# Neighbourhood attention: the probabilities are normalised by VectorE's tensor_scalar with an accumulated sum

## The chip, the cores and the metric

The kernel runs on one core of one Trainium2 chip. The metric is the time of one execution on the device in microseconds (us). Matmuls run on TensorE (PE in the profile, its weight loads PEld), elementwise work on VectorE (DVE), ScalarE (ACT) and GpSimd (POOL), and transfers are issued mostly by SyncE (SP). Matmul results land in PSUM, everything else lies in the on-chip buffer SBUF.

## The reference

Two layers of a transformer with two parallel mixers. Each layer projects the normalised and modulated tokens (512 latent tokens on a grid of 8 rows by 64 columns, and 256 context tokens) by one matrix, and runs two attentions of 8 heads each; both are gated, projected, merged and projected again. The change touches the first of the two, the neighbourhood attention, in which a latent query reads a window of 8 rows by 16 columns around it, and all 256 context keys:

```python
s_win = jnp.einsum('bchd,bicjhd->bhcij', qr, kw).astype(jnp.float32) * scale + bias[None]
s_ctx = jnp.einsum('bchd,blhd->bhcl', qr, kc).astype(jnp.float32) * scale
s = jnp.concatenate([s_win.reshape(B, NA_HEADS, GRID_W, wr * WIN_C), s_ctx], axis=-1)
p = jax.nn.softmax(s, axis=-1).astype(v.dtype)
```

The output is p times the values. In layer 0 the context tokens have queries too, which read the 256 context keys by an ordinary softmax; in layer 1 they have none.

## The kernel before, in words

All is fp32. A projection splits both factors into a high part that the fast matmul form keeps exactly and a low remainder, and multiplies three times: high by high, high by low, low by high (`mm3`, L435 to L437). The split of the weights costs a cast on ScalarE (L405, L420) and a subtraction on GpSimd or VectorE (L408, L422).

The neighbourhood attention goes head by head, 8 heads in a layer (`pipeline`, `na_first`, `na_scores`). For a head, keys and queries are staged first: `stage_k` (L866 to L868; the low part of the keys, `kl`, on GpSimd) and `stage_q` (L877 and L878; the low part of the queries, `qs`, on VectorE from two operands in SBUF). Then come four blocks of 128 queries by 512 columns, 256 for the window and 256 for the context. In each of them

- two matmuls give the scores in PSUM (L884, L885, or L972),
- VectorE adds the bias, negates, and writes the minimum beside the tile into the first column of `mx` (L975); its bias tile holds zeros in the context half,
- ScalarE takes the exponential and writes its sum into `r` (L978),
- `softmax_tail` turns `r` into its reciprocal on VectorE (L788) and multiplies p by it and by the constant P_UP = 2^14. For blocks 0 and 2 VectorE does both in one instruction over the tile (L795). For blocks 1 and 3 (NA_ACT) VectorE multiplies the 128x1 `r` by P_UP (L790), and ScalarE multiplies the tile (L793),
- `turned` splits the context half into two fp16 parts, on ScalarE (L835) and GpSimd (L836), and a transposing transfer of SyncE (L840) turns them.

Layer 0 has one more piece for each head: `ctx_scores` with `late` False, 2 x 128 context queries by 256 keys, which calls `softmax_tail` for two columns of `r` and two pieces of 256 columns, always on VectorE (two L795 for one L788). The call with `late` True, in the second attention, doesn't normalise there.

One head behind, `na_values` multiplies by the values: the window halves of p are turned on TensorE (L803, L805), evacuated in two fp16 parts (`transpose_split`, L811 on ScalarE and L812 on VectorE), and multiplied (L996 to L1006); `head_out` adds the two halves of the result (L825, L826) and multiplies it into the gate tile on GpSimd (L827).

Between the heads, `pipeline` runs pieces of gate projections (`fill`), which are matmuls of the `mm3` kind with their evacuations (L623, L625). They need nothing of the attention, and keep TensorE at work while a softmax is under way.

The order of the instructions on each engine is not the order of the code: the tile framework's planner lists them by its own estimate of when each could start, after the whole program is known. Some short runs are held together by hand (`behind`). An engine then works through its own list strictly in order.

The pool tiles concerned are `p` (8 buffers), `mx` (128x2, 8 buffers) and `r` (128x2, 8 buffers).

Of the kernel before, what the change touches and what calls it, by code (L numbers as in the profile page):

```python
# [12 lines left out]
ALU = mybir.AluOpType  # L13
# [20 lines left out]
NA_ACT = (1, 3)  # L34
P_UP = 2.0 ** 14
# [37 lines left out]
def hybrid_kernel(es: ExitStack, tc, x, ctx, cvec, w_ada, w_ada0, small, gvec, w_in, w_o_a, w_o_b, w_out,  # L73
                  bias_int, bias_edge, rope, ident_d, out):
    nc = tc.nc
    V, S, G, T = nc.vector, nc.scalar, nc.gpsimd, nc.tensor
# [10 lines left out]
    def nm(s):  # L87
        uid[0] += 1
        return f"{s}_{uid[0]}"
# [398 lines left out]
    def run(fill, n):  # L488
        for _ in range(min(n, len(fill))):
            fill.pop(0)()  # L490
# [102 lines left out]
    def layer(l, hx, nxt, start):  # L593
# [189 lines left out]
        bgp_es.close()  # L783

        if True:
            def softmax_tail(p, n, r, pieces, on_act=False):

                V.reciprocal(r, r)  # L788
                if on_act:
                    V.tensor_scalar(r, r, P_UP, None, ALU.mult)  # L790
                for i, (c0, c1) in enumerate(pieces):
                    if on_act:
                        S.activation(p[:, c0:c1], p[:, c0:c1], AF.Copy, scale=r[:, i:i + 1])  # L793
                    else:
                        V.tensor_scalar(p[:, c0:c1], p[:, c0:c1], r[:, i:i + 1], P_UP, ALU.mult, ALU.mult)  # L795

            def transpose_split(blocks, n0=0, n1=512):

# [30 lines left out]
            def turned(p, n, out, eng):  # L829

                if att["w"] == 512 and n == 512:
                    h = att["p"].tile([128, 2, n], F16, tag="hc", name=nm("hc"), bufs=1)
                else:
                    h = att["p"].tile([128, 2, n], F16, tag="h", name=nm("h"), bufs=att["nh"])
                S.copy(h[:, 0], p[:, :n])  # L835
                eng.tensor_tensor(h[:, 1], p[:, :n], h[:, 0], ALU.subtract)  # L836
                if not isinstance(out, list):
                    out = [(out, 0, 128)]
                for o, n0, n1 in out:
                    nc.sync.dma_start_transpose(o, h[n0:n1].rearrange("p a n -> p (a n)"))  # L840
# [40 lines left out]
            def scores(ps, q, kh, kl, cuts):  # L881

                for c0, n, sl in cuts:
                    T.matmul(ps[:, c0:c0 + n], q, sl(kh), start=True, stop=False)  # L884
                    T.matmul(ps[:, c0:c0 + n], q, sl(kl), start=False, stop=True)  # L885

            def cut(a, b):
                return lambda k: k[:, a:b]

            def ctx_scores(q, kh, kl, ct, late=True):  # L890

                pss = ps_score()
                for i in range(2):
                    scores(pss, q[:, 512 + 128 * i:640 + 128 * i], kh, kl,
                           [(256 * i, 256, cut(512, 768))])
                mx = sp.tile([128, 2], F32, tag="mx", name=nm("mx"), bufs=8)
                V.tensor_reduce(mx, pss.rearrange("p (i n) -> p i n", i=2), AX, ALU.max, negate=True)
                if late:
                    V.tensor_scalar(mx, mx, P_LOG, None, ALU.add)
                p = p_tile()  # L900
                r = sp.tile([128, 2], F32, tag="r", name=nm("r"), bufs=8)
                for i in range(2):
                    S.activation(p[:, 256 * i:256 * i + 256], pss[:, 256 * i:256 * i + 256], AF.Exp,
                                 bias=mx[:, i:i + 1], accum_out=r[:, i:i + 1])
                if not late:
                    softmax_tail(p, 512, r, [(0, 256), (256, 512)])
                turned(p, 512, ct.rearrange("p a i k n -> p (a i k) n"), G)
                return ct, r

# [13 lines left out]
            def p_tile():  # L923
                return att["p"].tile([128, att["w"]], F32, tag="p", name=nm("p"), bufs=att["np"])

            def ps_score(n=512):
                return psw(n, "s")
# [18 lines left out]
            def load_bias(h):  # L946
                nc.sync.dma_start(bint[:, 0:256], bias_int[l, h])
                for i in range(2):
                    nc.sync.dma_start(bedg[64 * i:64 * i + 64, 128 * i:128 * i + 128],
                                        bias_edge[l, h, 64 * i:64 * i + 64])  # L950
# [3 lines left out]
            def na_scores(h, q, kh, kl):  # L954
                load_bias(h)
                ps_ = []
                ht = turns[:, 2048 * (h % 2):2048 * (h % 2) + 2048].rearrange("p (g n) -> p g n", g=4)
                for i in range(4):
                    pss = ps_score()
                    qi = q[:, 128 * i:128 * i + 128]  # L960
                    if i == 0:
                        scores(pss, qi, kh, kl, [(0, 128, cut(0, 128)), (128, 384, cut(384, 768))])
                    else:
                        o = 128 * (i - 1)
                        step = 512 - o

                        def sl(k, o=o, step=step):
                            a = k[:, o:o + 256]
                            return bass.AP(tensor=a.tensor, offset=a.offset,
                                           ap=[a.ap[0], [step, 2], [1, 256]])  # L970
                        for kk, b in ((kh, True), (kl, False)):
                            T.matmul(pss.rearrange("p (s n) -> p s n", s=2), qi, sl(kk), start=b, stop=not b)  # L972
                    p = p_tile()
                    mx = sp.tile([128, 2], F32, tag="mx", name=nm("mx"), bufs=8)
                    V.tensor_tensor_reduce(p[:, :512], pss, bedg if i == 0 else bint, -1.0, 3e38,  # L975
                                           ALU.add, ALU.min, mx[:, 0:1])
                    r = sp.tile([128, 2], F32, tag="r", name=nm("r"), bufs=8)
                    S.activation(p[:, :512], p[:, :512], AF.Exp, bias=mx[:, 0:1], scale=-1.0,  # L978
                                 accum_out=r[:, 0:1])
                    softmax_tail(p, 512, r[:, 0:1], [(0, 512)], i in NA_ACT)  # L980
                    at = [(0, 64, 0), (448, 512, 64)] if i == 0 else [(128 * i - 64, 128 * i + 64, 0)]
                    turned(p[:, 256:512], 256, [(ht[:, :, a:b], n, n + b - a) for a, b, n in at], G)
                    ps_.append(p)
                    run(att["bg"], 1)
                return ps_, ht
# [46 lines left out]
            def na_first(h):  # L1032
                j, e = h // 2, h % 2
                kh, kl = akt[e]
                stage_k(kav[:, j, :], e, kh, kl, False)
                q = stage_q(qav[:, j, :], e)
                st = na_scores(h, q, kh, kl)
                if not first:
                    return st, None
                o = 4096 + 1024 * (h % 2)  # L1040
                ct = turns[:, o:o + 1024].rearrange("p (a i k n) -> p a i k n", a=2, i=2, k=2)
                return st, ctx_scores(q, kh, kl, ct, False)
# [126 lines left out]
            def gq_first(h):  # L1169
                kh, kl = gkt[h // 4]  # L1170
                q = stage_q(qbv[:, h // 2, :], h % 2)
                ht = gq_scores(q, kh, kl)
                if not first:
                    return ht, None
                if h % 2 == 0:
                    ct = vbig[:, 2432:2944].bitcast(F16).rearrange("p (a i k n) -> p a i k n", a=2, i=2, k=2)
                else:
                    ct = att["p"].tile([128, 2, 2, 2, 128], F16, tag="ct", name=nm("ct"), bufs=1)
                return ht, ctx_scores(q, kh, kl, ct)
# [336 lines left out]
```

## Time and profile before

| | us |
|---|---|
| median of three runs | 1127.05 |
| the three runs | 1122.82, 1127.42, 1127.05 |
| the profiled execution, its own time | 1125.0 |
| the profiled execution, first to last instruction (span) | 1122.9 |
| neighbourhood attention of layer 0 in it, about | 150 to 285 |
| neighbourhood attention of layer 1 in it, about | 770 to 880 |

The mean granted TensorE clock of the profiled execution is 0.992 of full speed. A row of a group reads: line, engine, operation, tile written <- tiles read, shapes, count, then busy us, mean ns of one, and the idle time of the engine before them with what ended it. A row of the order of time reads: start, duration, engine, line, and in brackets the idle time before it with what ended it. An instruction's duration may overlap the next one's by a little, so the distance from one start to the next (the step) is often shorter than the duration.

### The profile page before, as it was taken

What the parts mean: (1) busy time and instruction counts of PE and PEld (TensorE: products, weight loads), DVE (VectorE), ACT (ScalarE), POOL (GpSimd) and SP (SyncE); (2) the same over time, 40 slices, a digit from 0 to 9 for tenths busy, and PEclk for the clock granted to TensorE, in tenths of its full rate; (3) what the DMA queues carried; (4) which work ended last, traced back from release to release, by engine and by line L of the source; (5) the groups of instructions that cost most, each with busy time, mean ns of one, the idle gap of its engine ahead of it and who ended that gap; (6) DMA issues with size and microseconds to landing.
All of it is one profiled execution on the core that took longest, in us unless ns stands there. A gap on an engine that the chain in (4) does not pass through costs nothing. (4 is left out here: it accounts for less than half of the span.)

```text
span 1122.9 us, 16871 instructions
## 1 busy us (share of the span) xinstructions
PE 1079.4 (96%) x5672; PEld 876.5 (78%) x5672; DVE 761.7 (68%) x1496; ACT 616.7 (55%) x1236; POOL 497.0 (44%) x413
## 2 busy tenths in 40 slices
PE   8999998999999999969999999999999999999998
PEld 5687887888888877757788788888776888776677
DVE  5667889874377478775577785466987565677473
ACT  6464278876333566655330275445997346777431
POOL 1044355655247244454521445233665473564531
PEclk9999998999999999989999999999999999999999
DMA  9454324555543497769524542453556436879742
GB/s 369 150 169 143 91 70 95 137 136 124 170 127 127 127 203 187 170 183 263 181 96 126 178 132 81 138 162 94 118 134 144 136 111 165 205 229 229 196 146 80
DMA packets 235999, 171.79 MB, mean 153 GB/s; under 512 B 160140, under 2 KB 201864, under 8 KB 234248
## 3 DMA queue, kind: packets, MB, share of 16 engines
q1 hardware_dynamic: 228576, 156.31, 51.5%
q0 software_dynamic: 2368, 7.87, 2.2%
q10 hardware_dynamic: 4968, 6.53, 1.8%
q8 instruction: 45, 0.74, 0.3%
q14 instruction: 42, 0.34, 0.1%
HBM read 115.58 MB, written 17.32 MB: 118 GB/s over the span
## 5 line engine op out<-in xcount | busy, mean ns | idle before, releaser
L836 POOL TENSOR_TENSOR h<-p,h 128x256 f16<-128x256 f32 (+2 forms) x104 | 112.5, 1090 | 144.3 <-ACT h L835 106.7
L435 PE MATMUL psf<-hx,whi 128*128 128x512 f32 (+1 forms) x360 | 137.8, 383 | 1.2 <-ACT zt L623 1.2
L422 POOL TENSOR_TENSOR wlo<-raw,whi 128x512 fp32r<-128x512 f32 x70 | 97.4, 1396 | 93.8 <-ACT whi L420 55.9
L437 PE MATMUL psf<-hx,wlo 128*128 128x512 f32 (+1 forms) x360 | 135.2, 376 | 0.0
L436 PE MATMUL psf<-hx,whi 128*128 128x512 f32 (+1 forms) x360 | 135.1, 375 | 0.0
L435 PE MATMUL psx<-whi,hx 128*128 128x512 f32 (+1 forms) x328 | 120.9, 372 | 0.0
L437 PE MATMUL psx<-whi,hx 128*128 128x512 f32 (+1 forms) x328 | 120.1, 367 | 0.0
L436 PE MATMUL psx<-wlo,hx 128*128 128x512 f32 (+1 forms) x328 | 119.6, 366 | 0.0
L420 ACT CAST whi<-raw 128x512 fp32r<-128x512 f32 x136 | 82.0, 619 | 62.8 <-DMA raw<-in_w_in_dram 40.3
L408 POOL TENSOR_TENSOR wlo<-raw,whi 128x512 fp32r<-128x512 f32 x40 | 59.6, 1493 | 123.9 <-ACT whi L405 78.1
L405 ACT CAST whi<-raw 128x512 fp32r<-128x512 f32 x88 | 54.5, 624 | 104.6 <-PE psx L437 34.2
L506 POOL TENSOR_TENSOR ss<-ss,ehalf 128x8 f32<-128x8 f32 (+2 forms) x40 | 63.1, 1580 | 79.4 <-DVE ss L503 74.2
L422 DVE TENSOR_TENSOR wlo<-raw,whi 128x512 fp32r<-128x512 f32 x66 | 69.5, 1054 | 36.5 <-ACT whi L420 35.0
L835 ACT CAST h<-p 128x256 f16<-128x256 f32 (+2 forms) x136 | 81.3, 616 | 11.4 <-DMA ct<-h 5.1
L1147 DVE CUSTOM_DVE_ANT_0 p<-pss,vb 128x768 f32<-128x768 f32 x64 | 60.3, 954 | 27.3 <-PE pss L885 23.8
L435 PEld LDWEIGHTS psf<-hx,whi 128*128 128x128 f32 x360 | 67.9, 188 | 13.6 <-ACT zt L623 2.3
L1148 ACT ACTIVATE p<-pss,mx 128x768 f32<-128x768 f32 x64 | 57.6, 900 | 36.1 <-DVE mx L1147 35.1
L437 PEld LDWEIGHTS psf<-hx,wlo 128*128 128x128 f32 x360 | 67.8, 188 | 12.0
L436 PEld LDWEIGHTS psf<-hx,whi 128*128 128x128 f32 x360 | 67.9, 189 | 10.5
L437 PEld LDWEIGHTS psx<-whi,hx 128*128 128x128 f32 x328 | 62.0, 189 | 10.3
L436 PEld LDWEIGHTS psx<-wlo,hx 128*128 128x128 f32 x328 | 62.0, 189 | 9.5
L435 PE MATMUL psx<-hx,whi 128*128 128x256 f32 (+1 forms) x208 | 69.0, 332 | 0.0
(337 smaller groups left out, 2986.2 us busy)
## 6 DMA issues: line engine op xcount, KB each, us to landing
raw<-in_w_in_dram SPq DMA_DIRECT2D x168, 256.0 KB, 3.0
rawb<-in_w_ada_dram SPq DMA_DIRECT2D x48, 256.0 KB, 2.7
raw<-in_w_out_dram SPq DMA_DIRECT2D x32, 256.0 KB, 2.9
tg<-gs SPq DMA_DIRECT2D x4, 1536.0 KB, 6.9
rawx<-in_w_ada_dram SPq DMA_DIRECT2D x4, 1024.0 KB, 10.3
rawy<-in_w_ada_dram SPq DMA_DIRECT2D x4, 1024.0 KB, 9.8
gs<-zt ACTq DMA_DIRECT2D x16, 256.0 KB, 2.7
raw<-in_w_o_a_dram SPq DMA_DIRECT2D x16, 256.0 KB, 3.1
```

The lines of the kernel that those rows point to most:

```text
L405: S.copy(hi[:, :n], raw[:, :n])
L408: e.tensor_tensor(lo[:, :n], raw[:, :n], F(hi[:, :n]), ALU.subtract)
L420: S.copy(hi, raw)
L422: lo_eng(i).tensor_tensor(lo, raw, F(hi), ALU.subtract)
L435: T.matmul(ps, lhs[0], rhs[0], start=first, stop=False)
L436: T.matmul(ps, lhs[0], rhs[1], start=False, stop=False)
L437: T.matmul(ps, lhs[1], rhs[0], start=False, stop=last)
L506: G.tensor_tensor(ss, ss, ehalf[:, :n], ALU.pow)
L835: S.copy(h[:, 0], p[:, :n])
L836: eng.tensor_tensor(h[:, 1], p[:, :n], h[:, 0], ALU.subtract)
L1147: V.tensor_tensor_reduce(p, pss, lift, -1.0, 3e38, ALU.add, ALU.min, mx[:, 0:1])
L1148: S.activation(p, pss, AF.Exp, bias=mx[:, 0:1], accum_out=r[:, i:i + 1])
```

## The change

`softmax_tail` gets the tile `mx` as one more argument, called `total`. Where VectorE normalises, the constant P_UP no longer stands in the instruction over the tile: `r` is multiplied by it beforehand, by the small instruction that the calls for ScalarE already had. The instruction over the tile multiplies by `r` and adds 0.0, and its form also writes the sum of what it writes along the row into the second column of `mx`, which nothing reads. Nothing else differs; blocks 1 and 3 are as they were.

```diff
-            def softmax_tail(p, n, r, pieces, on_act=False):
+            def softmax_tail(p, n, r, total, pieces, on_act=False):
 
                 V.reciprocal(r, r)
-                if on_act:
-                    V.tensor_scalar(r, r, P_UP, None, ALU.mult)
+                V.tensor_scalar(r, r, P_UP, None, ALU.mult)
                 for i, (c0, c1) in enumerate(pieces):
                     if on_act:
                         S.activation(p[:, c0:c1], p[:, c0:c1], AF.Copy, scale=r[:, i:i + 1])
                     else:
-                        V.tensor_scalar(p[:, c0:c1], p[:, c0:c1], r[:, i:i + 1], P_UP, ALU.mult, ALU.mult)
+                        V.tensor_scalar(p[:, c0:c1], p[:, c0:c1], r[:, i:i + 1], 0.0, ALU.mult, ALU.add,
+                                        accum_out=total[:, 1:2])
...
                 if not late:
-                    softmax_tail(p, 512, r, [(0, 256), (256, 512)])
+                    softmax_tail(p, 512, r, mx, [(0, 256), (256, 512)])
...
-                    softmax_tail(p, 512, r[:, 0:1], [(0, 512)], i in NA_ACT)
+                    softmax_tail(p, 512, r[:, 0:1], mx, [(0, 512)], i in NA_ACT)
```

## The prediction

> **What bounds the kernel now.** I read the page's first part, then the busy time by stretches of the two places where the changed function runs, then TensorE's waits there, and last the order of time around the longest of them.
>
> ```profile
> span 1122.9 us, 16871 instructions
> PE 1079.4 (96%) x5672; PEld 876.5 (78%) x5672; DVE 761.7 (68%) x1496; ACT 616.7 (55%) x1236; POOL 497.0 (44%) x413
> 150.00:285.00 135.00, 131.24 (x791) 111.56 (x790) 103.94 (x229) 104.40 (x238) 79.72 (x81) 0.97 0.51 120
> 770.00:880.00 110.00, 103.29 (x534) 80.12 (x533) 86.26 (x191) 89.32 (x191) 64.14 (x58) 1.00 0.51 129
> ```
>
> The first two lines are the page's; the other two are stretches (start and end, length, then busy time of PE, PEld, DVE, ACT, POOL, granted clock, share and rate of DMA): the neighbourhood attention of layer 0 and of layer 1. TensorE bounds the kernel: it is busy for 96% of the span. VectorE's time counts only where it makes TensorE wait or lose its clock. In these two stages TensorE has 135.00 - 131.24 = 3.8 us and 110.00 - 103.29 = 6.7 us without a matmul: all that the change can win at once.
>
> Next, the changed instruction (L795), by shape and by its longest wait; the last line stands under "who waited for it":
>
> ```profile
> L795 DVE TENSOR_SCALAR p<-p,r x48: 340/487/3866, 155.6 to 861.3; 128x512 f32<-128x512 f32 x32, 128x256 f32<-128x256 f32 x16
> L795 DVE TENSOR_SCALAR p<-p,r 128x512 f32<-128x512 f32 x32 | 26.9, 842 | 1.0
> L795 DVE TENSOR_SCALAR p<-p,r 128x256 f32<-128x256 f32 x16 | 7.1, 488 | 0.2
> 150.00:285.00 135.00, 19.19 (x32) 0.97 0.51 120
> 770.00:880.00 110.00, 14.82 (x16) 1.00 0.51 129
>   PE pst L805: 3.2, 1
> ```
>
> Fastest, median and slowest are 340, 487 and 3866 ns, and the mean of the 512-wide ones, 842 ns, is far above their median: some of them stand still in the middle. (The two rows of stretches count L795's VectorE time alone.) What they stand still for shows in the order of time, of VectorE, GpSimd and TensorE:
>
> ```profile
> 178.21 4.13 DVE L795 TENSOR_SCALAR p<-p,r 128x256 f32<-128x256 f32 x2
> 178.10 1.58 POOL L827 TENSOR_TENSOR za<-za,ho 64x512 f32<-64x512 f32 x1 [3.00 <-DMA bedg<-in_bias_edge_dram]
> 179.66 1.16 POOL L836 TENSOR_TENSOR hc<-p,hc 128x512 f16<-128x512 f32 x1
> 180.78 1.27 POOL L422 TENSOR_TENSOR wlo<-raw,whi 128x512 fp32r<-128x512 f32 x1
> 185.36 1.83 POOL L868 TENSOR_TENSOR kl<-ka,kh 64x768 fp32r<-64x768 f32 x1 [1.78 <-PE psf L437]
> 187.15 1.26 POOL L422 TENSOR_TENSOR wlo<-raw,whi 128x512 fp32r<-128x512 f32 x1
> 185.91 3.31 DVE L878 TENSOR_TENSOR qs<-qa,qs 64x768 fp32r<-64x768 f32 x1
> 203.05 0.95 DVE L878 TENSOR_TENSOR qs<-qa,qs 64x768 fp32r<-64x768 f32 x1
> 189.25 0.49 DVE L795 TENSOR_SCALAR p<-p,r 128x512 f32<-128x512 f32 x1
> 189.80 0.48 PE L805 MATMUL pst<-ident,p 128*128 128x128 f32 x1 [3.19 <-DVE p L795]
> 190.84 0.58 PE L996 MATMUL psv<-ht,va 128*128 128x512 f16 x1 [0.57 <-DVE r L790]
> 188.00:190.00 2.00, 0.20 (x1) 0.20 (x2) 1.97 (x3) 1.98 (x8) 0.41 (x1) 0.78 0.00 0
> 190.00:192.00 2.00, 1.43 (x4) 0.48 (x4) 1.97 (x8) 1.79 (x5) 1.13 (x2) 0.50 0.18 35
> 192.00:194.00 2.00, 2.00 (x11) 1.34 (x9) 2.00 (x3) 1.01 (x3) 1.75 (x3) 0.50 0.69 228
> 194.00:196.00 2.00, 2.00 (x12) 2.00 (x11) 1.97 (x8) 1.82 (x5) 1.52 (x3) 0.52 0.65 169
> 196.00:198.00 2.00, 2.00 (x18) 1.96 (x18) 0.91 (x2) 1.88 (x5) 1.40 (x3) 1.00 0.82 207
> ```
>
> (A row merges equal neighbours, hence 4.13 us for two.) L795 ends when three GpSimd instructions in a row have ended; then L878, with two operands in SBUF, is held by two more (3.31 us, against 0.95 us when nothing was in its way). The p that follows is late, TensorE stands for 3.19 us, then 0.57 us more, and the granted clock falls to 0.50 until 196. This stall costs 3.2 + 0.6 + (2.0 - 0.57) x 0.50 + 2.0 x 0.50 + 2.0 x 0.48 = 6.5 us, though only 3.8 us of it show as idle.
>
> **The change part by part.** *Removed:* the fast L795. Undisturbed, its step to the next instruction is 0.41 us at 512 columns, and a pair at 256 takes 0.53 us:
>
> ```profile
> 155.62 0.48 DVE L795 TENSOR_SCALAR p<-p,r 128x512 f32<-128x512 f32 x1
> 156.03 0.16 DVE L788 RECIPROCAL r<-r 128x1 f32<-128x1 f32 x1
> 156.22 0.15 DVE L790 TENSOR_SCALAR r<-r 128x1 f32<-128x1 f32 x1
> 156.29 0.41 DVE L625 SCALAR_TENSOR_TENSOR za<-za,psx 128x256 f32<-128x256 f32 x1
> 156.66 0.69 DVE L422 TENSOR_TENSOR wlo<-raw,whi 128x512 fp32r<-128x512 f32 x1
> 163.16 0.62 DVE L795 TENSOR_SCALAR p<-p,r 128x256 f32<-128x256 f32 x2
> 163.69 0.15 DVE L788 RECIPROCAL r<-r 128x1 f32<-128x1 f32 x1
> ```
>
> At medians of 0.487 and 0.340 us, layer 0's 16 + 16 would take 13.2 us and not 19.19, layer 1's 16 would take 7.8 us and not 14.82: 6.0 and 7.0 us are waiting.
>
> *Added, the form with a sum.* Its time isn't in this trace. The nearest rows are the mask-and-minimum of the same stage, which writes a minimum beside its tile and is followed by a read of it, and a reduction whose input lies in SBUF:
>
> ```profile
> 153.60 0.68 DVE L975 CUSTOM_DVE_ANT_0 p<-pss,bedg 128x512 f32<-128x512 f32 x1
> 154.22 0.08 DVE L975 DVE_READ_ACCUMULATOR2_ANT mx<- 128x1 f32 x1
> 154.22 0.68 DVE L975 CUSTOM_DVE_ANT_0 p<-pss,bint 128x512 f32<-128x512 f32 x1
> L503 DVE TENSOR_REDUCE ss<-sq 128x8 f32<-128x520 f32 x32 | 21.8, 688 | 7.0 <-ACT sq L502 6.8
> ```
>
> Below, the new form may stay at the step of 0.41 us; above, it takes 0.69 + 0.08 = 0.77 us one behind the other. I take 0.62, the step of L975 with its read, since that is the row that does the same two things: + 0.21 us each. At 256 columns the nearest is L625's step, 156.66 - 156.29 = 0.37, against 0.53 / 2 = 0.27: + 0.10 us. Layer 0: 16 x 0.21 + 16 x 0.10 = 5.0 us; layer 1: 16 x 0.21 = 3.4 us.
>
> *Added, the small multiply* (r by P_UP, L790's kind), once for each call that normalises on VectorE: 16 + 8 in layer 0, 16 in layer 1. L790's step is 0.07 us where the next instruction needs nothing of it. Here the next one reads r, and then a dependent step counts: 0.19 us, as from L788 to L790 above. 24 x 0.07 to 0.19 = 1.7 to 4.6 us, and 16 x 0.07 to 0.19 = 1.1 to 3.0 us.
>
> *What goes with it.* If the new form doesn't take what GpSimd holds, the 6.0 and 7.0 us of waiting go. VectorE's sum is then 5.0 + (1.7 to 4.6) - 6.0 = + 0.7 to + 3.6 us in layer 0, and 3.4 + (1.1 to 3.0) - 7.0 = - 2.5 to - 0.6 us in layer 1: neutral, with the gain where waits are long. The sum written into mx's second column has no reader; it is written behind both exponentials, on the engine that writes mx anyway. Queued behind L795 on VectorE are the next tiles' L975, for which ScalarE's exponentials wait. No DMA is added or moved.
>
> [...]
>
> *On TensorE.* Up to 182 us layer 0 has five L795 of 512 columns and four of 256, with seven multiplies: VectorE is 5 x 0.21 + 4 x 0.10 + 7 x (0.07 to 0.19) = 1.9 to 2.8 us longer, partly absorbed where it now waits. I let 1.3 us of it arrive. The two L795 at 178.21 take 4.13 us; without the wait they would take 0.74, so 3.4 us go. The stall of 3.2 us becomes about 3.2 - 3.4 + 1.3 = 1.1 us, too short for the clock to fall if it goes as with the stands of 0.6 and 0.8 us in layer 1:
>
> ```profile
> 813.17 0.33 PE L884 MATMUL pss<-kh,qs 128*128 128x128 f32 x1 [0.59 <-DVE mx L975]
> 814.63 0.44 PE L805 MATMUL pst<-ident,p 128*128 128x128 f32 x2 [0.80 <-ACT p L793]
> 814.00:816.00 2.00, 1.36 (x7) 1.21 (x8) 1.94 (x6) 1.95 (x3) 0.26 (x1) 1.00 0.33 106
> ```
>
> That is 6.5 - 1.1 = 5.4 us won (0 to 6.5). Layer 1: VectorE is 0.6 to 2.5 us shorter, and a part of 6.7 us idle follows it: 1.3 us won (0 to 6.7). Layer 0 after the stall: VectorE longer, TensorE mostly covered by the gate projections queued there: 0.5 us lost (0 to 3.6). Sum: - 5.4 - 1.3 + 0.5 = - 6.2 us.
>
> The profiled execution took 1125.0 us, 2.1 us more than its span, which stay: 1118.8. The median of the three runs is 1127.05, 2.05 above the profiled one; a median of the changed kernel I put as far above: 1120.9 us, 0.55% below. From no change a measurement of this kernel tells about 0.5%, 5.6 us.
>
> **The rivals.** *The wait is inherited* (no change). L878, L422 and the casts keep waiting for GpSimd: L878 lost 2.4 us soon after L795. If VectorE, earlier by 3.4 us, meets the next GpSimd run there, the same p is as late as now. For it: L878's two operands; against it: at 182 us GpSimd has just ended a run. It gives the old time within 2 us: 1126.
>
> *VectorE becomes late elsewhere* (slower). Place: layer 0, where VectorE is longer by up to 3.6 us, and where the order of each engine, written by a planner from its own prices, is written anew. Where a transposed p comes some 3 us behind TensorE's last other matmul, there is a second stall with half clock. Price: 6.5 us, the first stall being kept or replaced: 1127.05 + 6.5 = 1133.6. Against it: TensorE waits for VectorE only twice there now.
>
> [...]
>
> **How the numbers follow.** Forecast 0.40; wait inherited 0.25; late elsewhere 0.28; form unchanged 0.07, of which 0.05 stay within 0.5%. So faster 0.40, same 0.30, slower 0.30. The forecast alone: both gains whole and no loss, 6.5 + 6.7 = 13.2, gives 1113.9; no gain in layer 1 and 3 us of the stall's gain, 1124. The range goes from 1113 to 1134, which takes in the slower rival.
>
> **What would show it.** Right: L795's 512-wide instructions close together at 0.68 us with a read behind each, none above 1 us; L790 at 72; no 3 us wait of L805; the clock 1.00 throughout the stage in layer 0; TensorE's idle time there below 2 us. [...]

## The result, and the profile after

| | us |
|---|---|
| kernel before, beside it: median of 5 runs | 1126.37 (1122.82 to 1127.42) |
| changed kernel: median of 5 runs | 1120.12 (1118.72 to 1123.24) |
| ratio, 95% interval | 0.9957 [0.994, 0.9974] |
| changed kernel again, beside 29 runs of the kernel before: median of 12 | 1121.09 (1117.89 to 1124.67) |
| ratio, 95% interval | 0.9979 [0.9967, 0.9991] |

The change makes the kernel faster, by 4.8 us in the first comparison (0.0043 x 1126) and by 2.4 us in the second (0.0021 x 1124); both intervals hold 0.9967 to 0.9974. Below, a gain in us is always the ratio worked out in this way.

The page of the changed kernel, and the two stages of the neighbourhood attention in it (columns as before: length, PE, PEld, DVE, ACT, POOL, granted clock, DMA):

```profile
span 1121.5 us, 16967 instructions
PE 1080.5 (96%) x5672; PEld 879.5 (78%) x5672; DVE 760.4 (68%) x1584; ACT 617.7 (55%) x1236; POOL 501.5 (45%) x413
150.00:285.00 135.00, 130.66 (x793) 110.91 (x792) 104.11 (x284) 104.80 (x238) 81.99 (x81) 0.99 0.49 119
770.00:880.00 110.00, 103.24 (x532) 81.32 (x531) 85.47 (x223) 89.67 (x191) 64.36 (x59) 0.98 0.50 131
```

This execution took 1123.24 us, the longest of the five, so its trace is only 1.8 us below that of before (1125.0). VectorE's sums are as they were, 104.11 against 103.94 us in layer 0 and 85.47 against 86.26 in layer 1, although 48 reads and 40 multiplies have been added. The groups show what paid for them (line L795 of before is L794 here, L790 is L789):

```profile
L794 DVE TENSOR_SCALAR_CACHE_REDUCE p<-p,r x48: 467/733/748, 156.3 to 860.0; 128x512 f32<-128x512 f32 x32, 128x256 f32<-128x256 f32 x16
L794 DVE DVE_READ_ACCUMULATOR p<-p,r x48: 71/83/86, 157.0 to 860.7; 128x1 f32 x48
L794 DVE TENSOR_SCALAR_CACHE_REDUCE p<-p,r 128x512 f32<-128x512 f32 x32 | 23.7, 740 | 0.5
L794 DVE TENSOR_SCALAR_CACHE_REDUCE p<-p,r 128x256 f32<-128x256 f32 x16 | 7.6, 477 | 0.4
L789 DVE TENSOR_SCALAR r<-r x72: 127/153/515, 156.2 to 861.3; 128x1 f32<-128x1 f32 x64, 128x2 f32<-128x2 f32 x8
```

The operation has another name, a read stands behind each, and the slowest of the 48 takes 748 ns, where the old form's slowest took 3866: nothing stops it in the middle any more. The mean at 512 columns fell from 842 to 740 ns although the undisturbed instruction became longer.

What TensorE waited for in layer 0's stage (engine, tile, line <- what it waited for: us in total, times, longest):

```profile
PE psf L435 <- DVE zt L625: 1.8, 1, 1.8
PE psv L996 <- DMA bint<-in_bias_int_dram: 1.5, 1, 1.5
PE psx L435 <- DVE za L625: 0.9, 1, 0.9
```

The wait of 3.2 us on the normalised p is gone. In its place stands another, of a gate projection (L435) on VectorE's evacuation (L625), 34 us later. The order of time around it, of VectorE and TensorE, and the stretch behind it in which the granted clock is 0.50:

```profile
219.67 2.24 DVE L878 TENSOR_TENSOR qs<-qa,qs 64x768 fp32r<-64x768 f32 x1
222.50 0.48 DVE L794 TENSOR_SCALAR_CACHE_REDUCE p<-p,r 128x256 f32<-128x256 f32 x1
222.91 0.08 DVE L794 DVE_READ_ACCUMULATOR p<-p,r 128x1 f32 x1
223.03 0.48 DVE L794 TENSOR_SCALAR_CACHE_REDUCE p<-p,r 128x256 f32<-128x256 f32 x1
223.43 0.68 DVE L625 SCALAR_TENSOR_TENSOR zt<-zt,psf 128x512 f32<-128x512 f32 x1
224.17 0.50 PE L435 MATMUL psf<-hx,whi 128*128 128x512 f32 x1 [1.82 <-DVE zt L625]
224.80:228.21 3.41, 3.41 (x10) 2.64 (x9) 2.93 (x9) 1.91 (x6) 3.17 (x4) 0.50 0.65 165
```

L878 has two operands in SBUF and takes 2.24 us; two normalisations stand in VectorE's list behind it, and L625, for which TensorE waits, only behind these. The stand costs 1.82 us and the lower clock 3.41 x 0.50 = 1.7 us more: 3.5 us, where the removed one cost 6.5. The new stand is the prediction's second rival, at half the size. The old stand at 190 us is gone, but not by the predicted chain. At 178 us in this list GpSimd has nothing to do, so there is nothing that the normalisations could have waited for:

```profile
178.67 0.74 DVE L794 TENSOR_SCALAR_CACHE_REDUCE p<-p,r 128x512 f32<-128x512 f32 x1
179.79 1.30 POOL L422 TENSOR_TENSOR wlo<-raw,whi 128x512 fp32r<-128x512 f32 x1 [3.38 <-PE pss L885]
```

Whether the instruction's form or the planner's new order made each difference is what the experiments ask.

### The profile page after: what moved, and what is told of

Same layout as the page of the kernel before. It is cut to its first block, busy times and chain, and to the rows that moved or that the text cites. A ratio compares the mean times of both kernels' runs of the same rounds, so it can differ in the third digit from the quotient of the medians.

```text
span 1121.5 us, 16967 instructions
## 1 busy us (share of the span) xinstructions
PE 1080.5 (96%) x5672; PEld 879.5 (78%) x5672; DVE 760.4 (68%) x1584; ACT 617.7 (55%) x1236; POOL 501.5 (45%) x413
## 4 chain that ended last, share of the span: by engine, by line
PE 33%; issue 5%; DVE 5%; DMA 4%; ACT 3%; POOL 2%; SPq 0%; POOLq 0%; ACTq 0%; DVEq 0%
PE psx L437 6%; PE psx L436 6%; PE psx L435 6%; PE psf L436 3%; PE psf L435 3%; PE psf L437 3%; DMA raw<-in_w_in_dram 1%; DMA ht<-h 1%; POOL wlo L408 1%; DMA raw<-in_w_o_a_dram 1%; PE pst L527 1%; ACT p L1148 1%; PE pst L1164 1%; DMA rawb<-in_w_ada_dram 1%; PE pst L1165 1%
## 5 line engine op out<-in xcount | busy, mean ns | idle before, releaser
L836 POOL TENSOR_TENSOR h<-p,h 128x256 f16<-128x256 f32 (+2 forms) x104 | 112.8, 1093 | 149.6 <-ACT h L835 111.0
L422 POOL TENSOR_TENSOR wlo<-raw,whi 128x512 fp32r<-128x512 f32 x70 | 98.6, 1412 | 96.5 <-ACT whi L420 56.8
L435 PE MATMUL psf<-hx,whi 128*128 128x512 f32 (+1 forms) x360 | 138.2, 384 | 3.0 <-DVE zt L625 1.8
L435 PE MATMUL psx<-whi,hx 128*128 128x512 f32 (+1 forms) x328 | 120.9, 372 | 0.0
L422 DVE TENSOR_TENSOR wlo<-raw,whi 128x512 fp32r<-128x512 f32 x66 | 69.4, 1052 | 42.0 <-ACT whi L420 40.6
L435 PEld LDWEIGHTS psf<-hx,whi 128*128 128x128 f32 x360 | 68.2, 189 | 15.9 <-DVE zt L625 2.3
L435 PE MATMUL psx<-hx,whi 128*128 128x256 f32 (+1 forms) x208 | 68.9, 331 | 0.9 <-DVE za L625 0.9
```

What stands on the lines that cost most here:

```text
L422: lo_eng(i).tensor_tensor(lo, raw, F(hi), ALU.subtract)
L435: T.matmul(ps, lhs[0], rhs[0], start=first, stop=False)
```

## The experiments

Each ratio is to runs of the kernel before that were made beside it (median 1124.27 us for the two exchanges and the one-layer kernels, 1123.85 for the four kernels from the repetition to the copies planned in, 1123.88 for the last four exchanges). Some kernels were "planned anew": the planner wrote each engine's list for the changed program. In others the instruction's form was exchanged in the finished lists, so that every engine's list stays that of another kernel. In the diffs `outputs` is what the instruction writes; `...` marks lines left out.

**The form alone, in the list of before.**

```diff
 V.tensor_scalar(p[:, c0:c1], p[:, c0:c1], r[:, i:i + 1], P_UP, ALU.mult, ALU.mult)
-outputs: (p[:, c0:c1])
+outputs: (p[:, c0:c1], r[:, i:i + 1])
```

> The instruction list of the kernel before, engine by engine, with only the form of the 48 changed instructions exchanged after planning (the sum goes into the r that each has just read; no added multiply). In this form the tile is not multiplied by P_UP, so these blocks of p stay without that factor. Theory (the form frees VectorE from waiting for GpSimd): no 512-wide one above 0.8 us, the 3.2 us wait of TensorE near 190 us gone or below 1.2 us, time 1120 to 1122. Rival (the planner's new order made the gain, the form alone only costs): 48 slower instructions in the old order, 1126 to 1129.

This kernel leaves out the factor P_UP in these blocks of p. Measured: 1118.46 us, 0.9946 [0.9927, 0.9965], 6.1 us faster. The same place in its trace, in the order of time and in slices:

```profile
177.97 1.29 POOL L827 TENSOR_TENSOR za<-za,ho 64x512 f32<-64x512 f32 x1 [3.00 <-ACT pt L811]
179.47 1.18 POOL L836 TENSOR_TENSOR hc<-p,hc 128x512 f16<-128x512 f32 x1 [0.21 <-PE psx L437]
178.21 0.47 DVE L795 TENSOR_SCALAR_CACHE_REDUCE p<-p,r 128x256 f32<-128x256 f32 x1
178.61 0.73 DVE L795 TENSOR_SCALAR_CACHE_REDUCE p<-p,r 128x512 f32<-128x512 f32 x1
183.01 3.70 DVE L878 TENSOR_TENSOR qs<-qa,qs 64x768 fp32r<-64x768 f32 x1
186.74 0.75 DVE L795 TENSOR_SCALAR_CACHE_REDUCE p<-p,r 128x512 f32<-128x512 f32 x1
187.55 0.33 PE L805 MATMUL pst<-ident,p 128*128 128x128 f32 x1 [0.85 <-DVE p L795]
188.00:190.00 2.00, 1.40 (x10) 0.89 (x10) 1.96 (x11) 1.24 (x3) 1.37 (x3) 1.00 0.26 71
770.00:880.00 110.00, 103.23 (x553) 81.79 (x552) 83.97 (x209) 87.87 (x190) 62.17 (x59) 1.00 0.54 137
```

The two L795 at 178.21, which took 4.13 us together, now run through in 0.47 and 0.73 while GpSimd's L827 runs beside them (its L836 starts only behind them). L878 still waits (3.70 us), but it starts 2.9 us earlier, so TensorE stands for 0.85 us instead of 3.19 and its clock stays at 1.00. With every list held as it was, this is the predicted chain, link by link, and its predicted size (1.1 us left, 5.4 us won). The 1.3 us forecast for layer 1 don't show in this trace: TensorE is idle there for 110.00 - 103.23 = 6.8 us, as before (6.7).

**The reverse: the changed kernel's list, with the old form.**

```diff
 V.tensor_scalar(p[:, c0:c1], p[:, c0:c1], r[:, i:i + 1], 0.0, ALU.mult, ALU.add)
-outputs: (p[:, c0:c1], total[:, 1:2])
+outputs: (p[:, c0:c1])
```

> The instruction list of the changed kernel, engine by engine, with the second output of the 48 instructions taken off after planning, so that they are the fast form again; the small multiplies stay. Theory (the form frees VectorE from waiting for GpSimd): medians back at 0.49 us, but single ones above 1.5 us again; 1124 to 1128. Rival (the new order made the gain): 1117 to 1120, no slower than the changed kernel.

Measured: 1121.22 us, 0.9977 [0.9962, 0.9991], between the two times expected. It is level with the changed kernel's second comparison (0.9979) and 0.2% behind its first (0.9957), which its interval doesn't separate from it either (0.9962 to 0.9974 lie in both). Its normalisations, those at 178 us, TensorE's longest wait in layer 0, and the clock behind that:

```profile
L794 DVE TENSOR_SCALAR p<-p,r x48: 345/484/3341, 156.2 to 861.1; 128x512 f32<-128x512 f32 x32, 128x256 f32<-128x256 f32 x16
178.08 0.74 DVE L794 TENSOR_SCALAR p<-p,r 128x256 f32<-128x256 f32 x2
225.43 0.50 PE L435 MATMUL psf<-hx,whi 128*128 128x512 f32 x1 [2.00 <-DVE zt L625]
226.00:228.00 2.00, 2.00 (x6) 1.60 (x5) 1.80 (x5) 0.52 (x2) 1.90 (x3) 0.50 0.34 131
```

The new stand on L625 is there too, with 2.00 us. So it comes with the order, not with the form. And at 178 us the two normalisations in the old form take 0.74 us together, which is what the prediction gave them without a wait: the order alone had already taken away the stand that the form was to take away.

In this list too a normalisation stands still, for longest in layer 1 (3.34 us, with a median of 0.48). What it costs shows beside the changed kernel at the same place; the first two rows are of this kernel with the old form, the other three of the changed kernel:

```profile
833.59 3.34 DVE L794 TENSOR_SCALAR p<-p,r 128x512 f32<-128x512 f32 x1
838.56 0.50 PE L972 MATMUL pss<-kh,qs 128*128 128x512 f32 x1 [2.00 <-DVE mx L975]
833.11 0.75 DVE L794 TENSOR_SCALAR_CACHE_REDUCE p<-p,r 128x512 f32<-128x512 f32 x1
834.15 2.42 DVE L866 CAST kh<-ka 64x768 fp32r<-64x768 f32 x1
837.36 0.50 PE L972 MATMUL pss<-kh,qs 128*128 128x512 f32 x1 [1.41 <-DVE mx L975]
```

The new form runs through in 0.75 us, but the copy of the keys behind it (L866) now takes 2.42 us instead of 0.56. It ends at 836.57, 0.42 us after a run of three instructions of GpSimd (L836 twice and L422, from 833.62 to 836.15). The wait is inherited, as the first rival had it, and TensorE's stand shrinks by 0.6 us only.

**One layer at a time** (planned anew).

```diff
-                V.tensor_scalar(r, r, P_UP, None, ALU.mult)
+                fast = not first        # in the other kernel: fast = first
+                if on_act or not fast:
+                    V.tensor_scalar(r, r, P_UP, None, ALU.mult)
...
+                elif fast:
+                    V.tensor_scalar(p[:, c0:c1], p[:, c0:c1], r[:, i:i + 1], P_UP, ALU.mult, ALU.mult)
```

With `not first` only layer 0 has the new form, with `first` only layer 1.

> The change in layer 0 alone (multiply, form and sum), layer 1 as before. By the prediction's terms - 5.4 + 0.5 = - 4.9 us of the median before, 1126.4: 1121.5. Rival (the gain lies in layer 1): 1126. Rival (a planner's new order of layer 0 costs what the stall gives): 1126 with a lower clock at another place of layer 0.

> The change in layer 1 alone, layer 0 as before. By the prediction's terms - 1.3 us (0 to - 6.7): 1125.1, and layer 0 with the 3.2 us wait and the half clock as before. Rival (the gain lies in layer 1): 1120 to 1122.

Measured: layer 0 alone 1119.91 us, 0.9963 [0.9947, 0.9978], 4.2 us faster (the terms of the prediction said 4.9); layer 1 alone 1123.24 us, 0.9982 [0.9967, 0.9996], 2.0 us (1.3). In the second the old stand of layer 0 is in place, by the list of TensorE's waits (L805 of before is L809 here, L795 is L796):

```profile
PE pst L809 <- DVE p L796: 3.2, 1, 3.2
```

The two add up to 6.2 us, the changed kernel has 2.4 to 4.8; the intervals are too wide (each about 1.7 us either way) to call that a loss.

**The changed kernel again, the small multiply alone, and no multiply.** The second keeps the old form; the third leaves out the factor P_UP with its multiplies. Both were planned anew.

```diff
-V.tensor_scalar(p[:, c0:c1], p[:, c0:c1], r[:, i:i + 1], 0.0, ALU.mult, ALU.add, accum_out=total[:, 1:2])
+V.tensor_scalar(p[:, c0:c1], p[:, c0:c1], r[:, i:i + 1], 0.0, ALU.mult, ALU.add)
```

```diff
-P_UP = 2.0 ** 14
+P_UP = 1.0
...
-                V.tensor_scalar(r, r, P_UP, None, ALU.mult)
```

> The changed kernel once more, on the chip and beside the runs of the kernel before that the other three have, so that they can be set against it. Its ratio was 0.9957; the same is expected, 0.994 to 0.998.

> The added multiply without the form: r is scaled first, and the tile is multiplied by r in the fast form, planned anew. Theory (the gain is the form's): nothing is freed and 40 small instructions are added, 0 to 4 us slower than the kernel before. Rival (half of the gain is the order that the planner writes with the multiplies in it, as the changed list with the fast form gave 0.9977): 1 to 3 us faster than before.

> The changed kernel with P_UP set to 1, and without the small multiply in all blocks (72 small instructions fewer than the changed kernel): p is kept in its natural size before it is split into two fp16 parts. Theory (by the prediction's terms the multiplies cost VectorE 2.8 to 7.6 us, in part on the path): 0 to 3 us faster than the changed kernel. Rival (they lie beside other work, and the new order decides): within 1.5 us of the changed kernel, to either side.

Measured: again 0.9979 [0.9967, 0.9991]; multiply alone 1121.77 us, 0.9983 [0.997, 0.9997]; no multiply 1120.74 us, 0.9974 [0.9962, 0.9986]. The multiplies cost nothing that shows, though the planner's order differs in the third kernel as well. More telling is the second: it frees nothing and adds 40 instructions to VectorE, and is faster than before by 1.9 us, so through the order alone. Its stand on p in layer 0 is shorter than before's, and the clock is back earlier:

```profile
186.98 0.33 PE L804 MATMUL pst<-ident,p 128*128 128x128 f32 x1 [1.96 <-DVE p L794]
187.70:191.12 3.42, 3.42 (x16) 2.42 (x14) 3.35 (x8) 2.13 (x5) 2.50 (x4) 0.50 0.46 116
```

The profiled execution of the changed kernel from this second comparison has a span of 1116.1 us, against 1121.5 in the first: the same program, 5.4 us apart. Two of its stands:

```profile
223.37 0.50 PE L435 MATMUL psf<-hx,whi 128*128 128x512 f32 x1 [1.55 <-DVE zt L625]
858.28 1.04 PE L996 MATMUL pss<-ht,va 128*128 128x512 f16 x4 [1.89 <-DMA ht<-h]
```

In the first execution the second of these, a wait for a transposed part of p (L996), looked so:

```profile
862.31 1.17 PE L996 MATMUL pss<-ht,va 128*128 128x512 f16 x4 [2.73 <-DMA ht<-h]
863.09:866.50 3.41, 3.41 (x14) 2.96 (x13) 1.52 (x3) 2.58 (x7) 2.17 (x3) 0.50 1.02 311
```

With 1.55 and 1.89 us TensorE keeps its clock; with 1.82 and 2.73 it loses it, each time for 3.41 us at 0.50, which is 1.7 us. The longer stands add 0.27 and 0.84 us. That is 4.5 of the 5.4 us. The stands that the changed order leaves are of a length at which the clock falls in one execution and not in the next; the last section shows what decides it.

**The same form for the copy of the keys.** `stage_k`'s copy `kh` (L866) goes from SBUF to SBUF and waits for the same thing, as the 2.42 us above show; the 16 copies of the neighbourhood attention (those with `dup` False) get the form with a sum, into a column that nothing reads (planned anew).

```diff
-                V.tensor_copy(rows(kh, e), k)
+                if dup:
+                    V.tensor_copy(rows(kh, e), k)
+                else:
+                    V.tensor_scalar(rows(kh, e), k, 1.0, 0.0, ALU.mult, ALU.add, accum_out=rows(vsa[:, 3:4], e))
```

> The changed kernel with the same form also for the copy of the keys' high part in the neighbourhood attention (16 instructions of 64x768, 819 ns in the mean in the changed kernel, 0.54 us when undisturbed: 16 x 0.28 = 4.5 us of waiting). [...] Theory (the form pays only where the wait is longer than its own slowness): 0 to 3 us slower than the changed kernel. Rival (the freed GpSimd counts): 1 to 3 us faster.

Measured: 1113.37 us, 0.991 [0.9894, 0.9926], 10.1 us faster than before, more than either expectation had, and the fastest version that is planned in the ordinary way. The theory's 0 to 3 us slower was the author's estimate; a copy takes 943 ns in the mean, 124 more than in the changed kernel's first execution (819). Its two stages (the second over 765 to 875), and TensorE's longest wait in the first:

```profile
150.00:285.00 135.00, 133.86 (x813) 112.77 (x812) 103.45 (x292) 104.38 (x238) 81.46 (x81) 1.00 0.55 129
765.00:875.00 110.00, 106.90 (x573) 85.25 (x572) 88.56 (x236) 90.73 (x195) 62.88 (x60) 1.00 0.55 137
PE pss L887 <- DVE mx L978: 0.7, 1, 0.7
```

TensorE stands for 1.1 and 3.1 us in them, against 4.3 and 6.8 in the changed kernel, and the clock stays at 1.00. But is that the copies, or once more the order? Four exchanges in finished lists separate them:

```diff
 copies in the list of that kernel:       outputs: (kh, sum)  ->  (kh)
 softmax in the list of that kernel:      outputs: (p, sum)   ->  (p)
 copies in the changed kernel's list:     outputs: (kh)       ->  (kh, sum)
 copies and softmax in before's list:     outputs: (kh), (p)  ->  (kh, sum), (p, sum)
```

> The instruction list of the version that also gives the keys' copy the form with a sum (median 1113.4, ratio 0.991), with the 16 copies turned back to the fast form after planning; softmax keeps the new form. Theory 1 (freeing the copies' wait for GpSimd gained it): back to 1118 to 1121. Theory 2 (the list that the planner wrote gained it): stays at 1112 to 1115.

> The same list, with the 48 softmax instructions turned back to the fast form after planning; the copies keep the new form. Theory 1 (freed waits count, in this list as in the list of before, where the form alone gave 5.8 us): 3 to 6 us slower than that version, 1116 to 1120. Theory 2 (in a list in which TensorE does not wait, the form of softmax gives nothing): within 1.5 us of 1113.4.

> The instruction list of the changed kernel (ratio 0.9979 beside these runs' predecessors), with the 16 copies of the keys exchanged for the form with a sum after planning. Theory 1 (freed waits): 2 to 5 us faster than the changed kernel, ratio 0.993 to 0.996. Theory 2 (the list): no better than the changed kernel, 0.997 to 1.000, since each copy is longer by some 0.1 us in the mean.

> The instruction list of the kernel before with both exchanges made after planning, softmax and the copies of the keys; no multiply is added, and these blocks of p stay without the factor P_UP. With softmax alone it was 0.9946. Theory 1 (freed waits add up): 0.990 to 0.993. Theory 2 (softmax's form had already taken TensorE's one long wait away, so nothing is left to gain in this list): 0.994 to 0.997.

| list | softmax | copies | us | ratio |
|---|---|---|---|---|
| with copies planned in | sum | sum | 1113.37 | 0.991 [0.9894, 0.9926] |
| with copies planned in | sum | old | 1112.71 | 0.9899 [0.9885, 0.9912] |
| with copies planned in | old | sum | 1114.63 | 0.9919 [0.9905, 0.9932] |
| changed kernel's | sum | old | 1121.09 | 0.9979 [0.9967, 0.9991] |
| changed kernel's | sum | sum | 1117.76 | 0.9948 [0.9935, 0.996] |
| changed kernel's | old | old | 1121.22 | 0.9977 [0.9962, 0.9991] |
| before's | sum | old | 1118.46 | 0.9946 [0.9927, 0.9965] |
| before's | sum | sum | 1118.76 | 0.9954 [0.9942, 0.9967] |

(The two in before's list leave out the factor P_UP in these blocks of p.)

In the list with the copies planned in, turning the copies back loses nothing, and turning the softmax back loses 1.0 us by the ratios (0.991 to 0.9919), which the intervals don't tell from nothing. So no single exchange carries the 10 us there, and the list itself is the likely cause of most of them. That list with both turned back wasn't run; it would show whether one exchange stands in for the other.

In the changed kernel's list the copies' form is worth some 3.5 us (0.9979 to 0.9948), in before's, beside the softmax's, nothing. One reason shows at the place where the changed kernel's copy inherited the wait. With the copies' form exchanged as well, the same copy reads (L866 is L869 here):

```profile
830.02 0.95 DVE L869 TENSOR_SCALAR_CACHE_REDUCE kh<-ka 64x768 fp32r<-64x768 f32 x1
```

It takes 0.95 us instead of 2.42, and TensorE has no stand there at all. The softmax's form alone only hands the wait on to the next instruction; both together take it away. In the list with the copies planned in, the copies in the old form take 642 ns in the mean (847 in the second execution of the changed kernel), so there is little for their exchange to free. Why the planner's order with the copies in it leaves no long stand wasn't traced further.

## Why the prediction was right or wrong

*The number* was right in the first comparison (1120.9 forecast, 1120.12 measured; 1120.9 / 1127.05 = 0.9945 lies within [0.994, 0.9974]). The second comparison, with 2.4 us, leaves 0.9945 outside its interval. So the direction is firm, and the size of 6.2 us was too large by 1.4 to 3.8 us. That it came so near is in part luck: the sum was made up of a chain in before's list, and in the list that ran the old form has 0.9977 as well.

*The mechanism* was right, and is shown in before's list: the form doesn't wait for GpSimd (748 ns at most in the changed kernel, 750 in before's list, where the old one took 3866), the stand of 3.19 us becomes 0.85 (forecast 1.1), the clock stays, 6.1 us are won (5.4 + 1.3 forecast without multiplies; layer 1's idle time is unchanged). That the form would not wait was an assumption of the author's: no run of the kernel before has the form; these durations bear it out.

*The step that failed* is "Layer 0 after the stall: VectorE longer, TensorE mostly covered by the gate projections queued there: 0.5 us lost", and with it the signs "clock 1.00 throughout" and "TensorE's idle time there below 2 us". Measured: 3.5 us at 222 to 229 in the first execution, 1.6 in the second, and 135.00 - 130.66 = 4.3 us idle. The gate projections were no cover: the late one was itself a gate projection, waiting for its evacuation on VectorE. The prediction costed everything in before's order, but the planner wrote another, in which the old stand is gone even with the old form and another stands elsewhere. The second rival had named this and was given the full price of the old stall (6.5 us, the first one kept or replaced); what came was half of it, as a replacement, and so the kernel is faster rather than slower. In the changed list the gain of the form alone can't be told from zero by these runs (0.9957 and 0.9979 with it, 0.9977 without); how the 2.4 to 4.8 us divide between form and order stays open within that.

*The wait is inherited* was partly true: in before's list L878 did wait, 3.70 us, but from an earlier start; in the changed list the copy of the keys took the wait over at 834 us (2.42 us), and the form saved TensorE 0.6 us there. *Form unchanged*, the 0.07 of the forecast, is refuted: the longest of the 48 takes 748 ns against 3866, and the form's step at 512 columns is 0.67 us against 0.41.

*The terms:* the form's step at 512 columns is 0.67 us rather than 0.62 (from 156.35 to its read at 157.02), + 0.26 us each rather than + 0.21; at 256 it is 0.41 (222.50 to 222.91), + 0.14 rather than + 0.10. The 3.8 us without a matmul in layer 0 were not "all that the change can win at once": the prediction's own 6.5 us counts the lower clock too. The multiplies, 2.8 to 7.6 us of VectorE's time together, moved the end by nothing measurable (0.9974 without them, 0.9979 with them). VectorE's sums came out at + 0.2 us in layer 0 (forecast + 0.7 to + 3.6) and - 0.8 in layer 1 (- 2.5 to - 0.6).

## What to carry to other kernels

A wait that another form of an instruction removes is worth what stands behind it in the list that will run: look whether the next instruction would wait for the same thing. Where a planner writes the order, a change of one instruction's kind is two changes, and the second can be the larger: here the same exchange was worth from nothing to 6 us by the list, and a list without anything freed won 1.9 us. Exchange the instruction in the finished list, and put the old one back into the new list, before a gain is credited to the instruction. And profile a kernel more than once before a stand of some 2 us is priced: with the clock a stand of 1.82 us cost 3.5 here, without it one of 1.55 us only itself.

## What the runs showed of the hardware

In these traces, whether a stand costs TensorE's clock goes by where it lies on a grid of time. In each of the 14 profiled executions all changes of the granted clock lie a whole number of 3.413 us apart; in the changed kernel's first one they are at 224.80, 228.21, 491.04, 504.69, 863.09 and 866.50 us, which is 1, 77, 4, 105 and 1 of these steps. From 30 us to 15 us before the end, the clock fell 25 times, and in the step just before the fall TensorE was always idle for at least 1.79 us in sum. In the 4329 other steps at full clock it was idle for 1.70 us or less, but for one with 1.86. Some steps (columns as before, TensorE's busy time first): before the fall in the kernel before and in the changed kernel, and then steps that end without a fall, in the changed kernel's second execution, in the changed list with the old form, and two in the kernel with layer 1 alone, with the stand that they share; the last row is before a fall again, in before's list with both exchanges:

```profile
185.69:189.10 3.41, 0.92 (x6) 0.55 (x4) 3.38 (x3) 3.34 (x10) 2.72 (x2) 1.00 0.22 45
221.39:224.80 3.41, 1.59 (x8) 1.06 (x8) 2.58 (x8) 2.21 (x5) 2.11 (x3) 1.00 0.38 77
219.96:223.37 3.41, 1.86 (x14) 1.42 (x13) 3.22 (x8) 2.25 (x5) 2.35 (x3) 1.00 0.35 70
202.06:205.48 3.42, 1.76 (x15) 1.66 (x14) 3.33 (x8) 2.04 (x8) 1.10 (x2) 1.00 0.44 94
856.03:859.45 3.42, 2.71 (x19) 1.70 (x17) 2.91 (x8) 3.39 (x9) 1.75 (x2) 1.00 0.46 90
861.04 1.04 PE L1000 MATMUL pss<-ht,va 128*128 128x512 f16 x4 [2.31 <-DMA ht<-h]
859.45:862.86 3.41, 1.82 (x13) 1.39 (x14) 0.64 (x4) 2.98 (x7) 2.07 (x4) 1.00 0.64 174
184.36:187.78 3.42, 1.63 (x9) 1.00 (x8) 3.39 (x9) 2.81 (x10) 0.69 (x2) 1.00 0.11 19
```

The stand of 2.31 us is longer than the 1.82 us that cost the changed kernel its clock, but a step ends in it, and neither of its parts reaches 1.79 us. In the last row two short stands in one step, of 1.07 and 0.72 us, were together enough. So a stand much shorter than the 3.2 us from which the prediction argued can be enough, and the same program can lose its clock in one execution and not in the next. A fall lasts whole steps, one or four in the execution above: one step costs 3.41 x 0.50 = 1.7 us if TensorE works through it. The stall of the kernel before took two, with 3.41 - 2.14 = 1.27 us idle in the first of them:

```profile
189.10:192.51 3.41, 2.14 (x6) 0.84 (x7) 3.34 (x11) 2.78 (x8) 1.64 (x3) 0.50 0.26 71
```

The steps do not keep to the program's own times: in the changed kernel's two executions, 221.39:224.80 and 219.96:223.37 lie 1.43 us apart, while the matmul that ends the stand starts 0.80 us apart (224.17 and 223.37).

The form with a sum takes 740 ns at 512 columns and 477 at 256, so about 1.03 ns for each element of a row, (740 - 477) / 256, and 214 ns besides, with a read of 71 to 86 ns behind it that partly lies under the next instruction. It is slower than the old form undisturbed (487 and 340 ns), and the mean of the old one in this kernel at 512 columns was 842.
